# Summing 32,768 rows: where each partition's rows lie in HBM

## The chip, the cores and the metric

The kernel runs on one core of one Trainium2 chip. The metric is the time of one execution on the device, in microseconds (us), as the median of several runs. A profiled execution gives the trace from which the views below are taken.

## The reference

The input is a gradient of 32 x 1024 rows with 2048 float32 numbers each. The output is the sum over all rows, one number per column (the bias gradient of a linear layer):

```
batch, seq, dim = 32, 1024, 2048
grad_output = randn(batch, seq, dim) as float32          # 268.4 MB
out = sum(grad_output, axis=(0, 1)) as float32           # 2048 numbers
```

## The kernel before

The input is seen as `flat`, 32,768 rows of 8 KB in HBM. SBUF has 128 partitions, and every load puts `m` rows into each of them, so one load takes `128 * m` rows. Since the sum runs over all rows, it doesn't matter which partition gets which row.

The helper `load(m, dst, lane, ...)` only notes a load in a list. It takes the next block of `128 * m` rows of `flat`, with `at_row` as a running counter, and lets partition p read rows `p * m` to `p * m + m - 1` of this block. The list is then issued in order by SP (SyncE) in `issue` (L108), on one DMA queue. A load may carry a wait: on `vec`, counted up by VectorE when a part of the ring has been read, or on `used`, counted up by TensorE. `lane` is the semaphore that the landing raises.

The loads, in order:

- `head`: one row per partition (1 MB);
- 30 tiles (`TILES`) of 8 rows per partition, 8 MB each, into a ring of three slots in SBUF; from the fourth on, each waits until VectorE is done with the slot;
- 5 rows per partition (`rows_in`) and 4 rows per partition (`small_in`), into parts of the ring that are free again;
- four loads of one row per partition (`row_in`), each waiting for TensorE;
- the last two rows per partition, split by columns into 1536 (two loads) and 512 (two loads), so that the columns' sums can be finished one after the other.

The work on them: VectorE adds each tile into the ring in two additions of 128 x 8192 elements (`vadd`, L120), after `take` has waited for the tile's landing (L114). So 8 rows per partition become 4 partial rows, which are added into the next tile. The last tiles are folded down to one row per partition. TensorE adds across the partitions: a matmul with a column of ones (`matmuls`, L185) turns 128 partitions into one row in PSUM. It does this for the folded row and for the rows that come last and don't pass through VectorE; small extra matmuls (L202) run between these. ScalarE and VectorE copy the sums to SBUF (L216), and SP stores them in two parts.

What sets the order: SP's queue is in program order, VectorE and TensorE run their own programs, and semaphores written by hand tie them together. No planner moves anything.

Of the kernel before, what the change touches and what calls it, by code (L numbers as in the profile page):

```python
# [8 lines left out]
P = 128  # L9
# [7 lines left out]
TILES = 30  # L17
# [16 lines left out]
def kernel(  # L34
# [8 lines left out]
    flat = grad_output.rearrange("b s d -> (b s) d")  # L43
# [7 lines left out]
    ring = const_pool.tile([P, SLOTS * TILE * D], fp32)  # L51
# [9 lines left out]
    one, zero, vec, step, used, mm_left, mm_right, done = (tc.alloc_semaphore(n) for n in names)  # L61
# [11 lines left out]
    at_row = 0  # L73
    loads = []

    def load(m, dst, lane, after=None, first=None, lo=0, hi=D):
        nonlocal at_row
        if first is None:
            first = at_row
            at_row += P * m  # L80
        src = flat[first : first + P * m].rearrange("(p m) d -> p m d", p=P)[:, :, lo:hi]
        loads.append((dst.rearrange("p (m d) -> p m d", m=m), src, lane, after))

    load(1, head[:], head_in)
    for k in range(TILES):
        s = k % SLOTS
        load(TILE, rows(s * TILE, TILE), slot_in[s], (vec, k - 2) if k >= SLOTS else None)


    load(1 + LANES, rows(0, 1 + LANES), rows_in, (vec, TILES - 2))  # L90
    small_at = TILE
    load(SMALL, rows(small_at, SMALL), small_in, (vec, TILES - 1))
    for j in range(LANES):
        load(1, rows(j, 1), row_in[j], (used, j + 1))
    at = (small_at + SMALL) * D
# [3 lines left out]
    for lo, hi, pieces in ((0, cut, LEFT), (cut, D, RIGHT)):  # L99
        for j in range(LAST):  # L100
            n = hi - lo
            lane = last_in[len(final)]
            load(1, ring[:, at : at + n], lane, (vec, TILES - 1), at_row + j * P, lo, hi)
            final.append((at, lo, pieces, lane, j == LAST - 1))
            at += n

# [32 lines left out]
    with nc.vector.Fori(0, LOOPS):  # L139
        for s in (1, 2, 0):  # L140
            at, before = s * TILE, (s - 1) % SLOTS * TILE
# [20 lines left out]
    for k, to in ((TILES - 2, 2), (TILES - 1, 1)):  # L162
        at, before = k % SLOTS * TILE, (k - 1) % SLOTS * TILE
# [55 lines left out]
    for copy, half in ((nc.scalar.copy, 0), (nc.vector.tensor_copy, 1)):  # L219
        for i in range(2):  # L220
            lo, n, _ = LEFT[2 * half + i]
            result(copy, lo, n, (mm_left, len(LEFT)), left[half])
        lo, n, _ = RIGHT[half]
# [39 lines left out]
```

## Time and profile before

| | |
|---|---|
| median of 3 runs | 628.94 us (628.7 to 629.33) |
| the profiled execution | 628.72 us |
| its span (first to last instruction in the trace) | 626.9 us |
| VectorE busy | 533.2 us, 85% of the span |
| TensorE matmuls busy | 18.8 us |
| DMA packets, bytes | 5909, 268.46 MB |
| median from issue to landing, 30 tiles | 29.8 us |
| median from issue to landing, the four one-row loads | 9.2 us |

How to read it: the profiled execution is 1.8 us longer than its span, which is what lies around the instructions. In the views, DVE is VectorE, PE is TensorE, ACT is ScalarE, SPq is SP's own sequencer and L108 is line 108 of the kernel. The page cuts the span into 40 equal slices and gives a digit for each: the busy share in tenths. A row of the stretches has the start and end in us, the length, then busy time (and count) of PE, PEld, DVE, ACT and POOL, the granted TensorE clock, the mean busy share of the 16 DMA engines, and GB/s. A line of waits has total us, how many times, and the longest.

### The profile page before, as it was taken

The page shows a single profiled execution, that of the slowest core. Times are in us where ns is not written, and L with a number is a line of the kernel's source. Part 1 is how long each engine was busy: PE and PEld are TensorE (multiplying, and loading weights), DVE is VectorE, ACT ScalarE, POOL GpSimd, SP SyncE. Part 2 cuts the span into 40 slices and gives each one's busy share as a digit, 9 for nine tenths or more (in the row PEclk, how much of TensorE's full clock was granted, in tenths as well). Part 3 has the DMA queues.
Part 4 walks back from the last instruction along what each step waited for, and adds up shares of the span by engine and source line. Part 5 has one row for each costly group of instructions (what it writes and reads, how often), then busy time and mean ns, then how long its engine had stood idle before and what let it go on. Part 6 is the DMA issues. An engine that isn't in the chain of part 4 may idle for free. (4 is left out here: it accounts for less than half of the span.)

```text
span 626.9 us, 628 instructions
## 1 busy us (share of the span) xinstructions
PE 18.8 (3%) x160; PEld 6.9 (1%) x160; DVE 533.2 (85%) x70; ACT 2.8 (0%) x5; POOL 0.3 (0%) x5
## 2 busy tenths in 40 slices
PE   0000000000000000000000000000000000000056
PEld 0000000000000000000000000000000000000022
DVE  0349988889888898888988889988889888898995
ACT  0000000000000000000000000000000000000000
POOL 0000000000000000000000000000000000000000
PEclk9999999999999999999999999999999999999999
DMA  9999999999999999999999999999999999999997
GB/s 401 401 468 401 468 401 468 401 468 401 468 401 464 406 456 414 447 422 427 443 427 443 422 447 410 460 406 464 401 468 401 468 401 468 401 468 401 427 415 297
DMA packets 5909, 268.46 MB, mean 428 GB/s; under 512 B 658, under 2 KB 658, under 8 KB 1172
## 3 DMA queue, kind: packets, MB, share of 16 engines
q1 hardware_dynamic: 5908, 268.45, 99.1%
q8 instruction: 1, 0.02, 0.0%
HBM read 268.44 MB, written 0.01 MB: 428 GB/s over the span
## 5 line engine op out<-in xcount | busy, mean ns | idle before, releaser
L120 DVE TENSOR_TENSOR ring<-ring 128x8192 f32<-128x8192 f32 (+2 forms) x65 | 528.6, 8134 | 84.8 <-DVEq L114 82.0
L185 PE MATMUL psum<-ring,ones 128*1 128x352 f32 (+2 forms) x144 | 18.8, 496 | 598.9 <-DMA ring<-in_grad_output_dram 598.9
L185 PEld LDWEIGHTS psum<-ring,ones 128*1 128x1 f32 x144 | 6.5, 86 | 607.6 <-DMA ring<-in_grad_output_dram 600.7
L216 DVE COPY ring<-psum 1x352 f32<-1x352 f32 (+1 forms) x3 | 1.4, 486 | 5.1 <-PE psum L185 5.0
L202 PE MATMUL psum<-ring,ones 128*1 128x256 f32 x16 | 5.2, 410 | 6.1 <-PEq L114 6.1
L216 ACT COPY ring<-psum 1x416 f32<-1x416 f32 (+1 forms) x3 | 1.4, 453 | 620.6 <-PE psum L185 620.5
L120 DVE TENSOR_TENSOR ring<-ring,head 128x2048 f32<-128x2048 f32 x1 | 2.3, 2293 | 0.1
L133 DVE MEMSET psum<- 128x1024 f32 x1 | 0.9, 912 | 1.2 <-SPq L123 1.2
L202 PEld LDWEIGHTS psum<-ring,ones 128*1 128x1 f32 x16 | 1.2, 88 | 8.7 <-issue 8.0
L212 ACT ACT_TABLE_LOAD x1 | 1.3, 1283 | 0.9 <-SPq L123 0.9
L212 ACT COPY warm<-ones 1x1 f32<-1x1 f32 x1 | 0.2, 190 | 0.0
L247 POOL MEMSET const-bfloat16-1.0<- 128x1 bf16 x1 | 0.1, 102 | 0.0
L247 POOL MEMSET const-uint8-127<- 128x1 uint8 x1 | 0.1, 102 | 0.0
L127 POOL MEMSET ones<- 128x1 f32 x1 | 0.1, 100 | 0.5 <-SPq L123 0.5
L247 POOL MEMSET const-float32-0.0<- 128x1 f32 x1 | 0.1, 99 | 0.2 <-issue 0.2
L247 POOL MEMSET const-float32-1.0<- 128x1 f32 x1 | 0.1, 99 | 0.0
## 6 DMA issues: line engine op xcount, KB each, us to landing
ring<-in_grad_output_dram SPq DMA_DIRECT2D x1, 5120.0 KB, 22.6
ring<-in_grad_output_dram SPq DMA_DIRECT2D x1, 4096.0 KB, 14.7
ring<-in_grad_output_dram SPq DMA_DIRECT2D x4, 1024.0 KB, 9.2
ring<-in_grad_output_dram SPq DMA_DIRECT2D x2, 768.0 KB, 13.0
head<-in_grad_output_dram SPq DMA_DIRECT2D x1, 1024.0 KB, 4.9
ring<-in_grad_output_dram SPq DMA_DIRECT2D x2, 256.0 KB, 14.0
ring<-in_grad_output_dram SPq DMA_DIRECT2D x30, 29.8
out_dram<-ring SPq DMA_DIRECT2D x1, 6.0 KB
```

The costliest lines, as they stand in the source:

```text
L120: return nc.vector.tensor_add(out=rows(at, n), in0=rows(at, n), in1=other)
L127: nc.gpsimd.memset(ones[:], 1.0).then_inc(one, 1)
L133: nc.vector.memset(psum[:, : 2 * 512], 0.0).then_inc(zero, 1)
L185: mat = nc.tensor.matmul(sums[lo], lhsT=ones[:], rhs=ring[:, x : x + n], start=start, stop=then is not None)
L202: nc.tensor.matmul(psum[96:97, 2 * 512 : 2 * 512 + FILLER], lhsT=ones[:], rhs=rows(j, 1)[:, :FILLER], start=True, stop=True)
L212: nc.scalar.copy(out=warm[:], in_=ones[0:1, :])._wait_ge(one, 1)
L216: copy(out=res[:, lo : lo + n], in_=sums[lo])._wait_ge(*wait).then_inc(then, 1)
L247: nc = _bacc.Bacc("TRN2", target_bir_lowering=False, num_devices=1)
```

## The change

The input is seen as `share`, 128 partitions with 256 rows each. Partition p owns rows `256 * p` to `256 * p + 255`, which is 2 MB in one piece. A load of `m` rows per partition takes the next `m` rows of every partition's own piece, so `at_row` now counts rows of a partition (0 to 255) and no longer rows of the whole input. The contiguous run that a partition reads in one load has the same length as before (64 KB in a tile). Which loads there are, their sizes, destinations, waits and order stay as they were, and so does everything on the other engines.

```
+    share = flat.rearrange("(p r) d -> p r d", p=P)
+
     def load(m, dst, lane, after=None, first=None, lo=0, hi=D):
         nonlocal at_row
         if first is None:
             first = at_row
-            at_row += P * m
-        src = flat[first : first + P * m].rearrange("(p m) d -> p m d", p=P)[:, :, lo:hi]
+            at_row += m
+        src = share[:, first : first + m, lo:hi]
         loads.append((dst.rearrange("p (m d) -> p m d", m=m), src, lane, after))
...
-            load(1, ring[:, at : at + n], lane, (vec, TILES - 1), at_row + j * P, lo, hi)
+            load(1, ring[:, at : at + n], lane, (vec, TILES - 1), at_row + j, lo, hi)
```

## Prediction

> **What bounds the kernel now.** I read the page first, its slices and its table of DMA queues, because an engine count alone (DVE 85% busy) would name the wrong suspect.
>
> ```profile
> span 626.9 us, 628 instructions
> PE 18.8 (3%) x160; PEld 6.9 (1%) x160; DVE 533.2 (85%) x70; ACT 2.8 (0%) x5; POOL 0.3 (0%) x5
> DVE  0349988889888898888988889988889888898995
> DMA  9999999999999999999999999999999999999997
> q1 hardware_dynamic: 5908, 268.45, 99.1%
> HBM read 268.44 MB, written 0.01 MB: 428 GB/s over the span
> ring<-in_grad_output_dram SPq DMA_DIRECT2D x30, 29.8
> ```
>
> The DMA row is full in every slice but the last: all 16 DMA engines carry packets for 99.1% of the span. DVE, the busiest compute engine, has gaps in most slices. The input is read once, so bytes divided by rate is the time.
>
> Then the stretches, for the rate itself, and the timeline, for who waits inside one tile:
>
> ```profile
> 1.90:621.90 620.00, 16.91 (x144) 6.64 (x144) 531.18 (x67) 0.47 (x2) 0.00 (x0) 1.00 1.00 433
> 60.00:598.00 538.00, 0.00 (x0) 0.00 (x0) 484.93 (x58) 0.00 (x0) 0.00 (x0) 1.00 1.00 434
> 218.82 17.48 DVE L120 TENSOR_TENSOR ring<-ring 128x8192 f32<-128x8192 f32 x2 [1.88 <-DVEq L114]
> 238.17 17.48 DVE L120 TENSOR_TENSOR ring<-ring 128x8192 f32<-128x8192 f32 x2 [1.87 <-DVEq L114]
> ```
>
> The first line holds the whole stream: 620 us at 433 GB/s is 268.5 MB, all of the input. In the steady part the rate is 434 GB/s, or 27.1 GB/s for each of 16 engines; a 64 KB piece takes one engine 65,536 B / 27.1 = 2.42 us. In the timeline a tile comes every 238.17 - 218.82 = 19.35 us, which is 8 pieces per engine at 2.42 us. DVE needs 17.48 us of it and then waits 1.87 us for the next load (L114 is the wait in `take`). So **the DMA engines set the pace and DVE has 1.87 us to spare per tile.**
>
> Last, the chain of waits and SP's own waits, for the end of the program and for the issue of loads:
>
> ```profile
> 608.17 13.69 DMA ring<-in_grad_output_dram
> 621.87 0.04 issue
> 621.91 1.00 PE psum L185 x6
> SPq L108 <- DVE ring L120: 580.8, 29, 50.4
> ```
>
> The last load lands at 621.87, and what follows it (matmuls, copies, the stores) takes 626.9 - 621.9 = 5.0 us. SP's 580.8 us of waiting for DVE is a full queue, not a delay: up to three tiles may be outstanding, a tile lands a median 29.8 us after issue (a tile and a half), and the engines never run dry.
>
> [...]
>
> **The change part by part.**
>
> Instructions: the order of both kernels, engine by engine, is the same row for row: SP issues one head load of 128x2048, 30 loads of 128x16384, then 128x10240, 128x8192, four of 128x2048, two of 128x1536 and two of 128x512, with the same waits on `vec` and `used`. Nothing is added or removed on PE, DVE, ACT or POOL, and no wait moves. Cost: 0. Queues: SP's order is unchanged; nothing is moved past another DMA.
>
> Pieces: a tile load still gives each partition one contiguous run of 8 rows x 8 KB = 64 KB, so I expect the same count of packets and bytes (5909, 268.46 MB). Cost: 0. There is no saving either: the runs were as long before.
>
> Addresses: this is what changes. Before, the 128 pieces of a tile lie 64 KB apart in one block of 8 MB; after, they lie 2 MB apart over the whole 256 MB, all at the same offset within their 2 MB. For single-row loads the pitch goes from 8 KB to 2 MB. No row of the trace before shows it, so it is bounded from both sides:
> - Below: 0. The engines are at 27.1 GB/s each, so no gain; no loss if HBM can still supply 434 GB/s.
> [...]
> [...]
> [...]
>
> [...] Nothing covers this cost: the DMA row is the path that sets the end.
>
> Behind slower loads: DVE waits at L114 longer. [...] PE and ACT are waiting for most of the program anyway. The tail after the last landing, 5.0 us, stays.
>
> Sum, against the profiled execution: 809 (stream) + 626.9 - 620.0 = 6.9 (start and tail) + 1.8 (execution of 628.72 less its span of 626.9) = **818 us**. That execution is 0.2 us under the median of the runs, 628.94, which is less than the working is good for.
>
> **Rivals.**
>
> *No loss at all (not slower).* [...] this is a load that only reads, in 64 KB runs. [...] It decides from one point: HBM must supply 434 GB/s to these addresses. Then the DMA row is as before and the time 629. For it: [...] nothing in the before trace shows HBM under strain. [...] That the change doesn't alter the addresses as it says would end here too; the diff's view (128 partitions x 256 rows) leaves little room for that.
>
> *Only the short pieces suffer.* The 30 tiles keep their rate, and the loads in runs of 8 KB or less (head, four rows, the last two rows in parts: 7 MiB, 7.34 MB) lose [...]. They take 7.34 MB / 434 = 16.9 us[...], all of it at the program's ends where nothing hides it: 634 to 647. [...] I let this case reach to 700.
>
> *A harder collision.* [...]
>
> *Faster.* It needs more than 434 GB/s[...].
>
> **How the numbers follow.** About 0.2% (1.3 us) is what a measurement of this kernel can tell from no change. [...]700 to 950, likeliest at 818: 0.42. Short pieces or a mild loss, 634 to 700: 0.18. No loss: 0.16. Harder collision[...]: 0.21. Faster: 0.03. Faster 0.03, same 0.16, slower 0.42 + 0.18 + 0.21 = 0.81. The range starts at 628, to take in no loss, and ends at 1050, which adds some 0.05 of the harder case: 0.16 + 0.18 + 0.42 + 0.05 = 0.81.
>
> **What would show it right or wrong.** Right: the page after has the same instruction counts, about 5909 packets and 268.46 MB, [...]the DMA row still full (each packet lasts longer[...], rather than engines standing idle), DVE work still near 533 us[...]. Wrong by the first rival: tiles still 19.35 us apart. By the second: middle slices at 434 and a longer last slice. By the third: middle slices under 270 GB/s. If packet counts rise or some engines idle while others work, the cause is another than HBM addresses, and the prediction fails in its mechanism too.

## The result, and the profile after

The changed kernel takes 651.76 us (median of 6 runs, 650.11 to 653.57), before 628.96 us: ratio 1.0361, 95% interval 1.0339 to 1.0383. It is slower by 23 us, not by the 189 us of the forecast. Its profiled execution took 650.27 us with a span of 648.5 us, 21.6 us more than the span before (this execution is one of the fastest of the six; the medians differ by 22.8 us).

The page after: the span, the rows of DMA share and GB/s in 40 slices, the total, and the loads with their median us from issue to landing. The last line is the GB/s row of before.

```profile
span 648.5 us, 628 instructions
DMA  8999999999999999999999999999999999999995
GB/s 259 433 404 445 433 429 437 429 433 433 433 441 429 441 433 433 429 433 437 429 433 441 437 433 433 433 429 433 441 429 437 433 437 433 433 433 427 388 225 114
DMA packets 5909, 268.46 MB, mean 414 GB/s; under 512 B 658, under 2 KB 658, under 8 KB 1172
ring<-in_grad_output_dram SPq DMA_DIRECT2D x4, 1024.0 KB, 13.7
ring<-in_grad_output_dram SPq DMA_DIRECT2D x2, 768.0 KB, 24.0
head<-in_grad_output_dram SPq DMA_DIRECT2D x1, 1024.0 KB, 7.2
ring<-in_grad_output_dram SPq DMA_DIRECT2D x30, 29.8
GB/s 401 401 468 401 468 401 468 401 468 401 468 401 464 406 456 414 447 422 427 443 427 443 422 447 410 460 406 464 401 468 401 468 401 468 401 468 401 427 415 297
```

Instructions, packets and bytes are unchanged, as the diff says: only addresses differ. Then read the GB/s row from left to right: 259 in the first slice, about 433 from the fourth to the 36th, and 225 and 114 at the end, where before has 401 in the first slice and 415 and 297 in the last two. (In the middle 401 and 468 take turns before; their mean is that of the row after.) The loss sits at both ends. The tiles land 29.8 us after issue, as before; the head takes 7.2 us instead of 4.9, the four one-row loads 13.7 instead of 9.2, the loads of 1536 columns 24.0 instead of 13.0.

The stretches of the kernel after (columns as explained under the time and profile before; the last two are DMA share and GB/s), then two of before, its start and its last loads, say the same as rates:

```profile
0.00:31.30 31.30, 0.00 (x0) 0.00 (x0) 0.91 (x1) 1.47 (x2) 0.30 (x5) 1.00 0.91 335
100.00:574.00 474.00, 0.00 (x0) 0.00 (x0) 425.50 (x49) 0.00 (x0) 0.00 (x0) 1.00 1.00 433
617.50:643.80 26.30, 13.87 (x84) 4.70 (x84) 9.09 (x5) 0.99 (x2) 0.00 (x0) 0.74 0.89 193
...
0.00:25.30 25.30, 0.00 (x0) 0.00 (x0) 0.95 (x2) 1.47 (x2) 0.30 (x5) 1.00 0.97 414
608.20:621.90 13.70, 8.07 (x76) 3.46 (x76) 9.64 (x4) 0.00 (x0) 0.00 (x0) 1.00 1.01 417
```

The last stretch of after is the telling one: the engines carry packets for 89% of it, yet move 193 GB/s, where the same loads ran at 417 before. The engines are hardly idle; their packets take longer: one of 8 KB took 0.60 us on average in this stretch, 0.31 us in that of before.

The timeline gives the first addition and one tile of the middle, the chain of waits the last landing. The last line of each fence is the matching one of before:

```profile
31.34 8.69 DVE L123 TENSOR_TENSOR ring<-ring 128x8192 f32<-128x8192 f32 x1 [29.19 <-DVEq L117]
...
226.49 17.48 DVE L123 TENSOR_TENSOR ring<-ring 128x8192 f32<-128x8192 f32 x2 [1.90 <-DVEq L117]
245.85 17.48 DVE L123 TENSOR_TENSOR ring<-ring 128x8192 f32<-128x8192 f32 x2 [1.88 <-DVEq L117]
...
25.26 8.69 DVE L120 TENSOR_TENSOR ring<-ring 128x8192 f32<-128x8192 f32 x1 [23.11 <-DVEq L114]
```

```profile
606.15 2.94 PE psum L188 x13
...
617.51 26.29 DMA ring<-in_grad_output_dram
...
598.46 2.94 PE psum L185 x13
```

A tile in the middle still takes 245.85 - 226.49 = 19.36 us, and DVE still waits 1.9 us in it. The last landing is at 617.51 + 26.29 = 643.80. From these and the lines of before (its last landing, 621.87, stands in the prediction), the account of the 21.6 us:

| | before, us | after, us | loss, us |
|---|---|---|---|
| start to first addition on DVE | 25.26 | 31.34 | 6.1 |
| from there to the first matmul (30 tiles) | 573.20 | 574.81 | 1.6 |
| from there to the last landing (short loads) | 23.41 | 37.65 | 14.2 |
| from there to the end | 5.0 | 4.7 | -0.3 |

### The profile page after: what moved, and what is told of

It is laid out like the page before. It is cut to its first block, busy times and chain, and to the rows that moved or that the text cites. A ratio compares the mean times of both kernels' runs of the same rounds, so it can differ in the third digit from the quotient of the medians.

```text
span 648.5 us, 628 instructions
## 1 busy us (share of the span) xinstructions
PE 24.6 (4%) x160; PEld 8.1 (1%) x160; DVE 533.3 (82%) x70; ACT 2.8 (0%) x5; POOL 0.3 (0%) x5
## 5 line engine op out<-in xcount | busy, mean ns | idle before, releaser
L188 PE MATMUL psum<-ring,ones 128*1 128x352 f32 (+2 forms) x144 | 24.5, 620 | 608.1 <-DMA ring<-in_grad_output_dram 608.1
## 6 DMA issues: line engine op xcount, KB each, us to landing
ring<-in_grad_output_dram SPq DMA_DIRECT2D x4, 1024.0 KB, 13.7
ring<-in_grad_output_dram SPq DMA_DIRECT2D x30, 29.8
```

The lines of the kernel that those rows point to most:

```text
L188: mat = nc.tensor.matmul(sums[lo], lhsT=ones[:], rhs=ring[:, x : x + n], start=start, stop=then is not None)
```

## The theories

None of these is shown yet; the experiments decide.

**A, colliding addresses.** Engines that read at one offset within 2 MB at one moment slow each other. An engine that is slowed falls behind, so its offset moves away from the others'. In a run of 64 KB there is room for 16 engines at different offsets (the room is the length of address over which they can spread), and once they are spread, nothing collides. At the program's start they begin together, and in the short loads there is no room.

**B, distance.** Each change of partition goes to another 2 MB region and costs something, which long runs hide. **C:** short pieces alone suffer. **D:** the loss belongs to a program's start and end, where few loads are in flight.

The trace has a view that bears on A. In a stretch of 4.84 us in the middle (two rounds of 2.42 us in which each engine starts a 64 KB piece), the GB/s row counts a piece's bytes where the piece starts, so it shows how far apart the engines are in time. Before:

```profile
GB/s 542 0 4875 542 0 0 0 0 0 0 0 0 0 0 0 0 0 0 1083 1625 542 0 4875 542 0 0 0 0 0 0 0 0 0 0 0 0 0 0 1083 1625
```

After:

```profile
GB/s 542 542 1083 0 0 1083 1083 0 542 542 0 0 0 0 542 1083 1083 0 0 542 542 542 1083 0 0 1083 1083 0 542 542 0 0 0 0 542 1083 1083 0 0 542
```

One piece in a column is 542. Before, 16 pieces start within six neighbouring columns out of 20, nine of them in one: the engines go in step. After, the same 16 lie in 11 columns over the whole round. Something has pushed them apart.

The trace also holds the moment at which each of the 16 engines signals that its part of a tile has landed, and so a measure for every tile. Before, the last engine is 0.5 us behind the first in all 30 tiles. After, it is 1.7 us behind in the first tile, 2.8 to 3.0 in the next four and 3.2 to 3.3 from then on. And the price is seen where they start: the 64 KB pieces that begin in the first 12 us take 3.44 us on average after (29 pieces), 2.42 before (48).

## Experiments: is it the address, and which loads pay?

The ratios below are to the kernel before, measured again beside each run, with their 95% interval. The pitch is the distance between the places where neighbouring partitions begin to read. Edits are against the kernel after and shortened; "..." marks what is left out, and numbers stand for some names.

**255 rows.** One number, the pitch, is changed in the address:

```
-    share = flat.rearrange("(p r) d -> p r d", p=P)
...
-        src = share[:, first : first + m, lo:hi]
+        base = min(first, R - P * 255)
+        share = flat[base : base + P * 255].rearrange("(p r) d -> p r d", p=P)
+        src = share[:, first - base : first - base + m, lo:hi]
```

> Every load as in the kernel after, but partition p's piece starts 255 rows after its neighbour's, 2 MB less 8 KB (127 rows of the input are left out, as many read twice). Theory A, colliding addresses: partitions that read at one offset within 2 MB collide in HBM while their engines are in step; with 8 KB of skew per partition[...] they don't. Then everything comes back: 629 us (627.5 to 631), the first add at L123 or its line here near 25.3 us, the last six loads 13.7 us from the chain's last issue to landing. Theory B, distance: every change of partition goes to another 2 MB region and pays for that[...]. Then 255 rows are as bad as 256: 650 us (646 to 654).

Measured: 628.78 us against 628.78 us, ratio 1.0000 (0.9992 to 1.0009). All of it is back; its last loads, by the chain of waits:

```profile
609.62 12.66 DMA ring<-in_grad_output_dram
```

Partitions are as far apart as before this edit, less 8 KB, so **B falls**. And the view of starts in the middle, for this kernel:

```profile
GB/s 0 0 542 4875 1625 0 1625 0 0 0 0 0 0 0 0 0 0 0 0 0 0 0 542 4875 1625 0 1625 0 0 0 0 0 0 0 0 0 0 0 0 0
```

All 16 pieces start within five columns, and the last engine lands 0.4 to 0.6 us behind the first in every tile. Here the engines go in step at the full rate (433 GB/s in this stretch). In the kernel after, at 2 MB, the last engine ends up 3.2 to 3.3 us behind the first.

**The two mixes.** Only one class of loads is 2 MB apart, the other is in blocks as before (`SMALL` is 4 rows):

```
-        src = share[:, first : first + m, lo:hi]
+        if m >= SMALL:      # short_share: if m < SMALL
+            src = share[:, first : first + m, lo:hi]
+        else:
+            src = flat[P * first : P * (first + m)].rearrange("(p m) d -> p m d", p=P)[:, :, lo:hi]
```

> Loads of 4 and more rows per partition as after (2 MB apart), the head, the four one-row loads and the last two rows as before (one block each; some rows are left out, others read twice). From the trace after: of +21.6 us in the span, 6.1 come before the first add on VectorE, 1.6 between it and the first matmul, 14.2 in the last loads, -0.3 behind them. Theory A: the last loads are as before (-14.2), the head too (-2.3), the first tiles keep a loss since the engines start in step: 651.8 - 16.5 = 635 (632 to 638). Theory C, short pieces alone: 629 (628 to 630).

Measured: 632.95 us (ratio 1.0061, 1.0045 to 1.0078), +4.2. The timeline and, below it, the chain:

```profile
27.39 8.69 DVE L126 TENSOR_TENSOR ring<-ring 128x8192 f32<-128x8192 f32 x1 [25.24 <-DVEq L120]
...
67.53 17.48 DVE L126 TENSOR_TENSOR ring<-ring 128x8192 f32<-128x8192 f32 x2 [2.69 <-DVEq L120]
87.26 17.48 DVE L126 TENSOR_TENSOR ring<-ring 128x8192 f32<-128x8192 f32 x2 [2.25 <-DVEq L120]
106.60 17.47 DVE L126 TENSOR_TENSOR ring<-ring 128x8192 f32<-128x8192 f32 x2 [1.86 <-DVEq L120]
```

```profile
613.75 12.47 DMA ring<-in_grad_output_dram
```

The last loads are as before. The first addition is 2.1 us late, and DVE's waits shrink tile by tile, 2.69, 2.25, 1.86, until nothing is lost any more. The engines' landings spread at the same pace, 0.6, 1.1, 1.7 and 2.1 us in the first four tiles, and hold 2.1 to 2.7 from then on: the moving apart takes about four tiles. C alone (629) doesn't explain the 4.2 us.

> The opposite mix: the head, the four one-row loads and the last two rows with partitions 2 MB apart, the tiles and the loads of 5 and 4 rows in blocks as before (some rows are left out, others read twice). Theory A: 629 + 2.3 (head) + 14.2 (last loads) = 645.5 (642 to 649), last loads 26 us from last issue to landing. Theory C: all of it, 651 to 652. If the tiles are to blame for the late start of the tail, under 640.

Measured: 641.48 us (ratio 1.0201, 1.0184 to 1.0218), +12.7, a little under the expected 642 to 649; the head lands in 7.0 us, the last loads in 23.1 instead of the expected 26. The chain:

```profile
612.67 23.14 DMA ring<-in_grad_output_dram
```

So the short loads, 7 MiB of 256, carry the larger part. The two mixes add to 16.9 us, not 23.

> Tiles in blocks as before; everything else (head, 5 rows, 4 rows, four single rows, the last two) 2 MB apart (some rows are left out, others read twice). short_share, with 5 and 4 rows in blocks, took 641.5. If those two loads hold the missing part, 645 to 647; if it comes from the tiles that ran before (engines further apart in time), 641 to 643.

The edit is `if m < TILE` in the mix above. Measured: 641.65 us (ratio 1.0206, 1.0189 to 1.0223), so the loads of 5 and 4 rows add nothing. The missing 6 us arise only where tiles and short loads are both 2 MB apart. In the profiled executions they are 4.2 us: 1.1 up to the first matmul, 2.5 in the last loads, 0.6 behind them. How they arise, these runs don't show.

## Experiments: does it end because the engines move apart?

**One tile in flight.** Every tile waits for the one before, so that the engines begin each tile together (the control also has the blocks of the kernel before):

```
-        load(TILE, ..., slot_in[s], (vec, k - 2) if k >= SLOTS else None)
+        load(TILE, ..., slot_in[s], (vec, k - 1) if k >= 2 else None)
```

> Control for the next: blocks as before, but a tile's load waits until VectorE has made the first addition of the tile before (vec, k-1), so only one tile is in flight and all 16 engines start each tile together. A tile then costs its 19.35 us of transfer, one addition of 8.7 us and about 2 us of issue and landing, 30 us: 628.9 + 28 x 10.7 = 929 us (890 to 960) in any theory.

> As the control, but with partitions 2 MB apart. In the trace after, tiles run at 434 GB/s from about 70 us on; this asks why. Theory A: because the engines have moved apart, to different offsets in their 64 KB. Here every tile starts in step again and pays again what the first tiles paid in the kernel after, some 3.5 to 6 us each: 28 x 3.5 to 28 x 6 = 98 to 168 us over the control, plus the 14 of the last loads, so 1.11 to 1.20 of the control. Theory B[...]: no more than +25 us over the control (1.03).

Measured: the control 948.88 us (a tile comes every 30.7 us or so), ratio to before 1.5091 (1.5066 to 1.5116); with 2 MB 1021.3 us, ratio to before 1.6240 (1.6212 to 1.6267). The second is 1.076 of the first. By the table of loads the tiles of the control land in 21.9 us and those at 2 MB in 23.7; the control first:

```profile
ring<-in_grad_output_dram SPq DMA_DIRECT2D x30, 21.9
```

```profile
ring<-in_grad_output_dram SPq DMA_DIRECT2D x30, 23.7
```

Now every tile of the middle lands 1.8 us later, where the kernel after loses nothing. The account of the two spans (1019.9 and 947.2 us) closes: from the first addition to the one that releases the load of 5 rows 51.5, the start 4.8, the load of 5 rows 3.0, the last loads 14.4, what follows them -1.0, together 72.7 us. The recorded limit for B was +25 us. D isn't decided by this run, since few loads are in flight throughout. My size was too large (3.5 to 6 us per tile). The landings show that a tile which starts together on its own already spreads within its 8 pieces, by 0.9 to 2.3 us (0.4 to 0.9 in the control); that this is why it loses less is likely, not shown.

**Less room.** Each tile comes as 8 loads of one row, so all 128 pieces of a load are 8 KB at one offset of their 2 MB, whichever of them an engine takes. The queue stays full: up to three tiles are outstanding, as in the kernel after. The control has the pitch of 255 rows.

```
-        load(TILE, rows(s * TILE, TILE), slot_in[s], ...)
+        for i in range(8):
+            load(1, rows(s * TILE + i, 1), slot_in[s], ...)
...
-            take(nc.vector, slot_in[s])       # waits for 16
+            take(nc.vector, slot_in[s], 128)
```

> As the kernel after (2 MB apart), but each tile comes as 8 loads of one row, so an engine reads 8 KB in one partition and then the same 8 KB offset in the next. Theory A (engines move apart until their offsets don't collide): with 64 KB there is room for 16 engines at 4 KB distance, with 8 KB there is not, so the steady part stays slow, as the last loads of the kernel after: from 193 GB/s (its stretch from 617.5 to 643.8 us) to about 255, so 251.7 MB of tiles take 990 to 1300 us; 1000 to 1330 in all. Theory D (the loss is one of a program's start and end, where the queue is short): the steady part of 8 KB pieces is as in split8_255, 650 to 670.

> Control: the same 8 loads per tile, with partitions 255 rows apart (127 rows of the input are left out, as many read twice). In the trace before an 8 KB piece took about 0.32 us on its engine, 25.5 GB/s, 408 GB/s for 16, so 628.8 x 434 / 408 = 669 (650 to 680), whatever the theory.

Measured: 950.03 us at 2 MB (ratio 1.5126, 1.5060 to 1.5191) against 646.01 us at 255 rows (1.0272, 1.0255 to 1.0289). The stretch from 100 to 500 us, at 2 MB and then at 255 rows:

```profile
100.00:500.00 400.00, 0.00 (x0) 0.00 (x0) 241.10 (x28) 0.00 (x0) 0.00 (x0) 1.00 0.97 283
```

```profile
100.00:500.00 400.00, 0.00 (x0) 0.00 (x0) 349.50 (x41) 0.00 (x0) 0.00 (x0) 1.00 1.01 422
```

The same 16 engines, busy all the time (shares of 0.97 and 1.01), move 283 GB/s in place of 422, from first to last. **D falls**: with 8 KB of room the collision doesn't end. (Both estimates were somewhat high: 950 is just under the range of 1000 to 1330, and an 8 KB piece of the control took 0.31 us at the median, a little less than the 0.32 assumed.)

The engines drift apart here too. The last engine's part of a tile lands 2.2 us ahead of the first engine's first part of the next tile at the start, and 0.3 to 0.9 us ahead from the eighth tile on, where a load takes 3.7: they are apart by nearly a whole load and slow all the same.

Is it the room or the length of the piece? Two loads of every second row per tile have 8 KB pieces too, but each load takes four of them from every partition, spread over 56 KB (the trace doesn't show in which order an engine takes them):

```
+        for i in range(2):
+            src = share[:, base : base + TILE, :].rearrange("p (a b) d -> p b a d", b=2)[:, i]
```

> Pieces of 8 KB, 2 MB apart, but in two loads per tile of every second row: an engine reads four pieces of a partition, spread over 56 KB, before it goes to the next. Theory A: what counts is the room in which engines can move apart, not the length of a piece: near split8_255, and far from split8_share: 660 to 720. Theory C (short pieces suffer as such at this pitch): as split8_share.

Measured: 659.86 us (ratio 1.0492, 1.0475 to 1.0510), just under the expected 660 to 720; its last loads, 2 MB apart as in the kernel after, cost some ten of it (23.46 us against 13.28 in the control). The middle:

```profile
100.00:500.00 400.00, 0.00 (x0) 0.00 (x0) 349.32 (x41) 0.00 (x0) 0.00 (x0) 1.00 1.01 421
```

421 GB/s, as in the control. **C falls as a cause**: at this pitch, tiles in 8 KB pieces ran at 283 GB/s where a load covers 8 KB of each partition's 2 MB, and at 421 where its pieces are spread over 56 KB.

One rival stands. In split8_share an engine's own successive pieces of a load also lie at one offset. Whether its reads collide with those of other engines or with its own next ones, no run with 8 KB pieces separates, since each edit changes both. For pieces of 64 KB the runs point to other engines: short_block has the same pieces in every tile, loses in its first four, while the engines are 0.6 to 2.1 us apart, and nothing in the middle (433 GB/s).

**How much room.** Pieces of 16 and 32 KB (4 and 2 loads per tile), and 8 KB pieces at 1 MB:

> 2 MB apart, each tile as 4 loads of two rows: pieces of 16 KB[...] If room to move apart goes with the piece (8 KB gave 283 GB/s, 64 KB gave 433) and doubling it is enough, 425 to 434 GB/s and 655 to 670.

> 2 MB apart, each tile as 2 loads of four rows: pieces of 32 KB. Theory A: more room than 16 KB, so not slower than split4_share in its steady part; by the 4 KB per engine that 64 KB gives, some loss may stay at 2 KB: 652 to 680.

> 8 loads of one row per tile, partitions 128 rows (1 MB) apart (half of the input is left out, the other read twice). Is it 2 MB that collides, or any such distance? If 1 MB brings half of the streams to another place, their room doubles and it goes as split4_share; if 1 MB is like 2 MB, 950 (940 to 960); if it doesn't collide, 646 (644 to 650).

Measured: 657.61 us (1.0444, 1.0416 to 1.0472), 647.08 us (1.0281, 1.0264 to 1.0299) and 654.94 us (1.0421, 1.0404 to 1.0438). The stretches from 100 to 500 us, in this order:

```profile
100.00:500.00 400.00, 0.00 (x0) 0.00 (x0) 349.27 (x41) 0.00 (x0) 0.00 (x0) 1.00 1.00 422
```

```profile
100.00:500.00 400.00, 0.00 (x0) 0.00 (x0) 356.97 (x42) 0.00 (x0) 0.00 (x0) 1.00 1.00 432
```

```profile
100.00:500.00 400.00, 0.00 (x0) 0.00 (x0) 348.15 (x41) 0.00 (x0) 0.00 (x0) 1.00 1.01 420
```

Twice the room is nearly enough: 422 and 432 GB/s. At 32 KB I had expected more of the loss to stay (652 to 680 us). At 1 MB with 8 KB pieces it is 420, as if half the distance doubled the room; its start is slow (first addition at 31.08 us), its last loads are not (13.46 us). The prediction's 809 us for the stream would be 332 GB/s (268.4 MB in 809 us); pieces of 16 KB ran at 422.

**How far apart.** 8 KB pieces again, the pitch 2 MB less 1 KB and less 256 bytes, so that the pieces of a load differ in their offsets by 1 KB or 256 bytes from partition to partition:

```
+        row = R // P * D - SKEW               # SKEW = 256 or 64 numbers
+        cols = flat.rearrange("r d -> (r d)")[base : base + P * row].rearrange("(p e) -> p e", p=P)
```

> As split8_share (950 us), but partitions are 2 MB less 1 KB apart[...] (columns are shifted against each other, so the output is no column sum). [...] 646 (644 to 652). If the 8 KB[...] of the 255-row pitch were needed: 750 to 950.

> The same with 2 MB less 256 bytes[...] (columns shifted too). With 16 KB pieces, 16 engines found room at 1 KB each on average and ran near full rate (422 GB/s); if that distance is what counts, 646 to 665. If it takes more, near 950 (850 to 950)[...].

Measured: 652.38 us (1.0364, 1.0327 to 1.0402) and 786.79 us (776.89 to 795.71 in four runs; 1.2560, 1.2487 to 1.2634). The stretches, 1 KB of skew first:

```profile
31.30:100.00 68.70, 0.00 (x0) 0.00 (x0) 49.02 (x8) 0.00 (x0) 0.00 (x0) 1.00 1.01 393
100.00:500.00 400.00, 0.00 (x0) 0.00 (x0) 348.11 (x41) 0.00 (x0) 0.00 (x0) 1.00 1.01 421
```

```profile
100.00:500.00 400.00, 0.00 (x0) 0.00 (x0) 285.73 (x33) 0.00 (x0) 0.00 (x0) 1.00 1.00 347
```

With 1 KB per partition the middle is whole again (421 GB/s) and only the start pays a little (393 GB/s from 31.3 to 100 us; 652.38 us is at the edge of the expected 644 to 652); with 256 bytes the loss is roughly halved (the 347 is a mean: the rate rises from 334 at 100 to 200 us to 369 at 600 to 700 us). I had expected either end for 256 bytes; the loss is graded: 283, 347 and 421 GB/s at 0, 256 bytes and 1 KB. What distance two engines need, these runs don't show, since the trace doesn't say which partitions an engine serves.

**A version without the loss.** Each partition owns 255 contiguous rows, and the 128 rows left are the head load, in one block:

```
+    own = R // P - 1
+    share = flat[: P * own].rearrange("(p r) d -> p r d", p=P)
...
-    load(1, head[:], head_in)
+    loads.append((head[:], flat[P * own :], head_in, None))
```

> A whole sum, no row left out: each partition owns 255 contiguous rows (2 MB less 8 KB), and the last 128 rows of the input are the head load, one block. Theory A: 629 (628 to 630.5), no faster than before since the engines are at their rate of 434 GB/s. Theory B: 645 to 652.

Measured: 628.76 us against 628.77 us, ratio 0.9999 (0.9991 to 1.0008). It computes the whole sum, as fast as before and no faster: the middle runs at 433 GB/s in both. The last engine lands 0.2 to 0.3 us behind the first in every tile. None of these runs beats the kernel before.

## Why the prediction was right or wrong

- **What bounds the kernel: right.** The DMA engines do, before and after (a share of 1.00 and 433 GB/s in the middle), and no version with another layout had a median under 628.7 us.
- **No cost in instructions, pieces, queues and waits: right.** Packets, bytes and DVE's work (533.3 us) are the same.
- **Slower, because of the addresses: right.** 8 KB less of pitch takes all of the loss away (628.78 us in pitch_255). That a distance of 2 MB costs anything was my estimate; no trace of before showed it.
- **The term "addresses", 809 us for the stream: this step failed.** The figure was my estimate; no trace or run of this case stood behind it. It put one slower rate on the whole stream. The tiles, 251.7 MB of 268.4, keep 433 GB/s once the engines are spread, and what is lost is 6.1 us at the start, 1.6 up to the first matmul and 14.2 in the short loads, together with -0.3 behind them 21.6 us in place of 189. So the loss isn't a constant rate: the kernel after runs at 335 GB/s up to the first addition, 433 in the middle and 193 in the last loads. Nor do short pieces alone bring the forecast rate: tiles in 16 KB pieces ran at 422 GB/s, not 332.
- **The first rival (no loss)** was right for the tiles of the middle, in their runs of 64 KB (433 GB/s), and wrong at both ends: it forgot the start and the short loads.
- **The second rival (only the short pieces)** was nearest, at 634 to 647 for the short loads and up to 700 for a mild loss. Its 634 to 647, my estimate too, holds the 641.48 us of short_share; it left out the first tiles, +4.2 in short_block, and the 6 us that both together add. Its sign, middle slices at 434 and a longer last slice, is what the profile after shows in the main. It should have had most of the chance.
- **Longer waits of DVE in every tile: wrong** with the term above; the wait stayed at 1.9 us and the median 64 KB piece in the middle at 2.42 us. That the DMA row stays full because packets last longer came true at the ends alone.

What stays open: which part of HBM or of the way to it collides (no run looks inside), whether in 8 KB pieces an engine's own successive reads take part, and the 6 us that the two mixes leave.

## What to carry to other kernels

Before giving each partition its own contiguous share, look at the distance between shares: at 2 MB, reads in 8 KB pieces fell from 422 to 283 GB/s, and one row less (255 of 256) cured it at no cost (628.76 us against 628.77 in own_255). With tiles in pieces of 64 KB the loss didn't show in the steady part (433 GB/s) and stayed at the start (335) and in the short last loads (193), so read the GB/s row slice by slice, not its mean. A slowdown that no trace or run of the kernel at hand shows is to be tested and no forecast: at this one pitch it was 422 / 283 = 1.49 in 8 KB pieces, and 1.00 in the long ones of the middle.

## What the runs showed of the hardware that I had not expected

The DMA engines spread on their own at 2 MB. With tiles alone at that distance they lost 4.2 us over some four tiles (short_block), with the head and the first tile 6.1 us (the kernel after); from then on they stayed 2.1 to 3.3 us apart and ran at 433 GB/s until the last loads. At 255 rows they stayed within 0.6 us of each other to the end and lost nothing (628.78 us, as before). Once apart they stayed so: in short_share the head leaves them 1.75 us apart, and after 30 tiles in blocks they are still 1.75 us apart. Full DMA share says little of this: with 8 KB pieces the engines were busy 97% of the time at 283 GB/s and 101% at 422.
